# Projecting the neighbourhood queries ahead of keys and values in a two-block transformer kernel

## The chip, the cores and the metric

The kernel runs on one core of a Trainium2 chip, in one launch. The metric is the device time of that launch in microseconds; smaller is better. All arithmetic outside the tables of constants is done on the core, in float32 accuracy.

## The reference

Two transformer blocks follow each other on 256 tokens of width 1024. The first block (two layers) is not touched. The second block also has two layers, and it carries a second stream of 256 context tokens beside `x`. Shortened:

```python
for l in range(DEPTH):                      # 2 layers
    x     = swiglu_half_step(x, ...);  h_ctx = swiglu_half_step(h_ctx, ...)
    hx = modulate(rms_norm(x, ...), ...);  hc = modulate(rms_norm(h_ctx, ...), ...)
    px = hx @ w_in[l]
    pc = hc @ (w_in[l, :, Q_W:] if last else w_in[l])
    qa = rms_norm(heads(px[..., :NA_W]), ...)      # queries of the first kind, 8 heads
    qb = rms_norm(heads(px[..., NA_W:Q_W]), ...)   # of the second kind, 8 heads
    ...                                            # ka, va, kb, vb; the same of pc
    out_a = neighbourhood_attention(qa, ka, va, ka_c, va_c, na_rpb[l])
    out_b = windowed_gqa_attention(qb, kb, vb, kb_c, vb_c, wa_sink[l])
    x = x + mod_x[..., 5, :] * (jnp.concatenate([out_a, out_b], axis=-1) @ w_out[l])
    if not last:                                   # layer 0 alone
        ...                                        # both kinds on the context, into h_ctx
    x = swiglu_half_step(x, ...)
    if not last: h_ctx = swiglu_half_step(h_ctx, ...)
```

In the last layer the context gives keys and values and has no queries.

## The kernel before, in words

**Streams.** `x` and the context `c` are two Python generators, both instances of `stream` (L1511). While the program is recorded a planner (`main`, L1615) steps generators by a modelled clock: each yields a token (a weight product, a wait for an event, a point in time), the planner takes the one that is ready first, and of those ready together the one with the better priority. Smaller pieces run as generators of their own: `head_norm` (L1268) at priority `HN`, and the attention at priority `ATT`, 2 for `x` and 1 for `c`. The order in which they are stepped is the program order of every engine; on the chip nothing is reordered.

**Products.** A weight is loaded as a block `raw` of 128 output columns by 1024 (SyncE's queue), cast on ScalarE to `wh` and its rest kept as `wl` by VectorE (`split`, L148). I call the work on one such block a **unit**: 24 matmuls (8 of wh with the upper part of the activations, 8 of wl, 8 of wh with their lower part). Where both streams need a block at about the same time, one joint unit of 24 matmuls over 512 columns serves both (`together`, L236); otherwise each stream runs its own unit of 256 columns (`alone`, L226), from the same block held in memory. A joint unit takes about as long as two alone.

**The projections of a layer of block 2.** `w_in` has 8 units of queries (4 of the first kind, "kind 0", 4 of the second, "kind 1") and 6 of keys and values, called here by their place in the order of use, #1 to #14. `kv` (L1363) runs the 6 units, and spawns a `head_norm` of the keys; behind these it forms the values of kind 0. `qproj` (L1403) then runs the 4 units of kind 0, spawns their norm, and the 4 of kind 1, and spawns theirs. A head norm is a chain of short steps: squares, sums over heads by small matmuls with `c_heads`, a square root, transposes that spread the factors (`tr`), and for kind 1 of `x` a rotation by `c_rot`.

**Attention.** Behind `kv` a generator `attention` is spawned. It waits for keys and values (for `x` those of both streams), then for the queries of kind 0, runs that kind (`attend`, L829, with `attn2`, L1420), and then kind 1. For one head, ScalarE, VectorE and GpSimd cast keys and queries (`kk`, `qq`), PE forms the scores `ps_s`, ScalarE the exponentials `e` and their sums, PE transposes them (`ps_t`), `pt` copies them, and PE multiplies with the values (`ps_o`). Up to four heads are open (`DEPTH`). Then `w_out` (8 units, #1 to #4 need kind 0 alone) adds to the residual, and the next half step begins with `rms` (L624): sums of squares by small matmuls with `ones`, a square root, a spread, and the scaled activations `hmem`. Its first two units of `w_ffn_up` belong to #45 to #48 of that weight's order of use in the layer.

## Time and profile before

| | before |
|---|---|
| device time, median of 3 runs | 2626.09 us (2618.99 to 2626.55) |
| device time of the profiled execution | 2625.82 us, of which span 2624.0 us |
| TensorE matmul busy | 2491.1 us, 95% of the span |
| VectorE, ScalarE, GpSimd busy | 1743.6, 1046.2, 220.9 us |

The span runs from the first to the last instruction. Times in the trace count from the start of the span. Block 2's first half step and projections of layer 0 end, its attention begins, at about 1283 us; layer 1's attention begins at about 2317 us. "Clock" below is the TensorE clock granted by the throttle, as a share of full speed: 1.00 is 2.4 GHz, the other level is half of it, and a value between them is a mean over the stretch.

### The profile page before, as it was taken

Reading aid. Unit: us, or ns where it says so; the run is one execution under the profiler, and the core shown is the slowest. Engines: PE = TensorE matmul, PEld = TensorE weight load, DVE = VectorE, ACT = ScalarE, POOL = GpSimd, SP = SyncE. Lnnn points to the kernel's source line nnn. Section 1 sums busy time; section 2 is a strip of 40 time slices with the busy share of each in tenths; the row PEclk is TensorE's granted clock in tenths of the full one; section 3 lists DMA queues with packets and bytes.
Section 4 is the critical chain, followed back from the end, with each engine's and each line's share of the span. In section 5 each row is a group of like instructions: output and inputs, shape, how many; then the busy total and the mean of one; then the engine's idle time right before and its main releaser. Section 6 shows DMA issues by size and latency. Waiting matters only on the chain.

```text
span 2624.0 us, 40217 instructions
## 1 busy us (share of the span) xinstructions
PE 2491.1 (95%) x15668; PEld 2239.9 (85%) x15668; DVE 1743.6 (66%) x3255; ACT 1046.2 (40%) x1817; POOL 220.9 (8%) x243
## 2 busy tenths in 40 slices
PE   5989998999998999999989999999999999999999
PEld 4879998989997888889788888888888888988999
DVE  6788887588887765576666757465754445576754
ACT  3555444545443222233566322222322223365543
POOL 2111003121000000000252000000000000041000
PEclk9989998889998999999989899999999999989999
DMA  7776885546763644534311245454354443431564
GB/s 280 248 235 210 287 283 188 180 147 194 232 189 115 192 145 133 155 113 137 106 32 49 85 154 171 118 171 127 114 167 146 128 129 105 129 96 42 174 192 133
DMA packets 127071, 408.92 MB, mean 156 GB/s; under 512 B 15585, under 2 KB 21281, under 8 KB 126753
## 3 DMA queue, kind: packets, MB, share of 16 engines
q1 hardware_dynamic: 126880, 406.35, 49.4%
q8 instruction: 123, 2.02, 0.3%
q14 instruction: 68, 0.55, 0.1%
HBM read 405.22 MB, written 1.07 MB: 155 GB/s over the span
## 4 chain that ended last, share of the span: by engine, by line
PE 75%; DVE 11%; DMA 6%; ACT 4%; issue 3%; POOL 1%; SPq 0%; ACTq 0%; DVEq 0%; POOLq 0%
PE ps_mm L131 65%; PE ps_o L131 3%; PE ps_s L131 3%; DMA raw<-in_w_ffn_in 3%; DVE wl L149 3%; PE ps_t L136 2%; PE ps_t L131 2%; DVE junk L456 2%; ACT wh L149 1%; DMA raw<-in_w_ffn_out 1%; DVE hmem L653 1%; DVE tr L650 1%; DMA adaw<-in_w_ada 1%; POOL tr L475 1%; ACT e L785 1%
## 5 line engine op out<-in xcount | busy, mean ns | idle before, releaser
L131 PE MATMUL ps_mm<-hmem,wh 128*128 128x256 f32 (+1 forms) x5760 | 1386.3, 331 | 49.8 <-ACT hmem L473 21.6
L131 PEld LDWEIGHTS ps_mm<-hmem,wh 128*128 128x128 f32 x5760 | 997.0, 195 | 159.3 <-ACT hmem L473 22.0
L131 PE MATMUL ps_mm<-hmem,wl 128*128 128x256 f32 (+2 forms) x2880 | 950.9, 330 | 2.1 <-DVE wl L149 2.0
L149 ACT CAST wh<-raw 128x1024 fp32r<-128x1024 f32 (+2 forms) x572 | 546.0, 958 | 867.8 <-PE ps_mm L131 371.7
L149 DVE TENSOR_TENSOR wl<-raw,wh 128x1024 fp32r<-128x1024 f32 (+2 forms) x556 | 625.5, 1128 | 355.6 <-ACT wh L149 353.4
L131 PEld LDWEIGHTS ps_mm<-hmem,wl 128*128 128x128 f32 x2880 | 558.9, 194 | 49.9 <-DVE wl L149 2.9
L131 PE MATMUL ps_mm<-g,wh 128*128 128x256 f32 (+1 forms) x2328 | 534.1, 323 | 3.8 <-ACT g L149 3.8
L456 DVE SCALAR_TENSOR_TENSOR junk<-adaw,cb 128x1024 fp8e4<-128x1024 f32 x343 | 423.1, 1233 | 27.8 <-DMA adaw<-in_w_ada 23.3
L131 PEld LDWEIGHTS ps_mm<-g,wh 128*128 128x128 f32 x2328 | 393.0, 191 | 37.5 <-ACT g L149 4.0
L131 PE MATMUL ps_mm<-g,wl 128*128 128x256 f32 (+1 forms) x1164 | 375.3, 322 | 2.5 <-DVE wl L149 2.5
L131 PEld LDWEIGHTS ps_mm<-g,wl 128*128 128x128 f32 x1164 | 222.9, 191 | 19.3 <-DVE wl L149 2.9
L965 POOL TENSOR_TENSOR kk<-kT,kk 64x512 fp32r<-64x512 f32 (+1 forms) x30 | 35.7, 1189 | 1359.6 <-ACT kk L964 1358.5
L735 DVE TENSOR_TENSOR tr<-tr,ps_mm 128x512 f32<-128x512 f32 x61 | 42.0, 688 | 144.9 <-PE ps_mm L131 144.9
L734 ACT ACTIVATE tr<-ps_mm 128x512 f32<-128x512 f32 x61 | 36.5, 598 | 242.6 <-PE ps_mm L131 242.6
L756 DVE SCALAR_TENSOR_TENSOR x_res<-ps_mm,ada_x,x_res 128x256 f32<-128x256 f32 x144 | 67.0, 481 | 92.0 <-PE ps_mm L131 91.5
L131 PEld LDWEIGHTS ps_o<-g,pt 128*128 128x128 f32 x808 | 109.4, 207 | 11.2 <-ACT pt L371 7.4
L131 PE MATMUL ps_o<-g,pt 128*128 128x64 f32 (+1 forms) x808 | 111.8, 287 | 4.8 <-ACT pt L371 4.5
L785 ACT ACTIVATE e<-e,small 128x256 f32<-128x256 f32 (+2 forms) x160 | 90.7, 568 | 34.9 <-DVE small L779 33.8
L131 PE MATMUL ps_mm<-wh,hmem 128*128 128x256 f32 x512 | 94.1, 282 | 0.0
L136 PE MATMUL ps_t<-c_ident,e 128*128 128x128 f32 x404 | 69.8, 297 | 12.9 <-ACT e L785 5.8
L131 PEld LDWEIGHTS ps_mm<-wh,hmem 128*128 128x128 f32 x512 | 79.5, 188 | 0.6 <-ACT g L371 0.6
L149 ACT CAST g<-tr 128x256 fp32r<-128x256 f32 (+1 forms) x137 | 68.3, 499 | 25.2 <-DVE tr L681 10.9
(227 smaller groups left out, 2034.5 us busy)
## 6 DMA issues: line engine op xcount, KB each, us to landing
adaw<-in_w_ada SPq DMA_DIRECT2D x231, 512.0 KB, 4.4
raw<-in_w_ffn_up SPq DMA_DIRECT2D x176, 512.0 KB, 3.9
raw<-in_w_ffn_in SPq DMA_DIRECT2D x88, 512.0 KB, 4.6
raw<-in_w_ffn_down SPq DMA_DIRECT2D x96, 384.0 KB, 3.1
raw<-in_w_ffn_out SPq DMA_DIRECT2D x48, 384.0 KB, 4.0
raw<-in_w_in SPq DMA_DIRECT2D x28, 512.0 KB, 3.7
raw<-in_w_in_ab SPq DMA_DIRECT2D x16, 512.0 KB, 6.6
raw<-in_w_o SPq DMA_DIRECT2D x16, 512.0 KB, 4.8
```

What stands on the lines that cost most here:

```text
L131: self.tc.keep_in_program_order(self.nc.tensor.matmul(out, left, right, start=start, stop=stop))
L136: self.tc.keep_in_program_order(self.nc.tensor.transpose(out, in_, self.ident))
L149: return (self.nc.scalar.copy(hi, src), (eng or self.nc.vector).tensor_tensor(out=lo, in0=src, in1=hi.bitcast(F32), op=OP.subtract))
L456: ins = self.nc.vector.scalar_tensor_tensor(out=self.junk, in0=raw, scalar=1.0, in1=v, op0=OP.mult, op1=OP.mult, accum_out=acc[:, j:j + 1] ...
L475: nc.gpsimd.tensor_scalar(out=h32[:, j, :], in0=src[:, j, :], scalar1=a[:, k0 + j:k0 + j + 1], scalar2=b[:, k0 + j:k0 + j + 1], op0=OP.mul ...
L650: nc.vector.scalar_tensor_tensor(out=t[:, j, :], in0=x[:, k + j, :], scalar=a[:, k + j:k + j + 1], in1=bc, op0=OP.mult, op1=OP.mult)
L653: nc.vector.scalar_tensor_tensor(out=hl[:, k + j, :T], in0=t[:, j, :], scalar=b[:, k + j:k + j + 1], in1=hh[:, k + j, :T].bitcast(F32), op ...
L734: nc.scalar.activation(sg, job.full[0], AF.Silu)
L735: nc.vector.tensor_tensor(out=sg, in0=sg, in1=job.full[1], op=OP.mult)
L756: self.nc.vector.scalar_tensor_tensor(out=x[:, k, :], in0=ps[j], scalar=gate[:, k:k + 1], in1=x[:, k, :], op0=OP.mult, op1=OP.add)
L785: nc.scalar.activation(e[:, at:at + w], e[:, at:at + w], AF.Exp, bias=nm, scale=-1.0, accum_out=sm)
L965: self.nc.gpsimd.tensor_tensor(out=there, in0=k, in1=here.bitcast(F32), op=OP.subtract)
```

## The change

`qproj` takes the kind as an argument and projects that kind's 4 units only. `stream` calls it for kind 0 ahead of `kv`, and for kind 1 behind it, where the attention's generator has been spawned. The context of layer 1, which has no queries, skips both. The event `free`, on which attention pages wait, is set by `stream` behind the second call. No unit is added or taken away: in every shape the two programs have the same number of weight products.

```diff
@@ -1400,22 +1400,20 @@
         self.store[("v", th, l)] = (va, vb)
         self.events.add(("v", th, l))
 
-    def qproj(self, th, l):
-        self.store[("q", th, l)] = qs = []
-        for kind in range(2):
-            for ci in range(2):
-                job = yield from self.products(th, ("w_in_2", l), (4 * kind + 2 * ci, 4 * kind + 2 * ci + 1), self.h_mv,
-                                               ((0, KT),), l == 0)
-                sb = self.page("g")
-                if not job.full:
-                    self.copy(back(sb), rows(job.bank))
-                else:
-                    for j in range(2):
-                        self.copy(back(sb[:, j:j + 1, :]), rows(job.outs[j][:, None, :]))
-                qs.append(sb)
-            self.spawn(self.head_norm([(q, 2 * kind, kind == 1 and th == "x") for q in qs[2 * kind:]], l,
-                                      ("q", th, l, kind), True), HN)
-        self.events.add(("free", th, l))
+    def qproj(self, th, l, kind):
+        qs = self.store.setdefault(("q", th, l), [])
+        for ci in range(2):
+            job = yield from self.products(th, ("w_in_2", l), (4 * kind + 2 * ci, 4 * kind + 2 * ci + 1), self.h_mv,
+                                           ((0, KT),), l == 0)
+            sb = self.page("g")
+            if not job.full:
+                self.copy(back(sb), rows(job.bank))
+            else:
+                for j in range(2):
+                    self.copy(back(sb[:, j:j + 1, :]), rows(job.outs[j][:, None, :]))
+            qs.append(sb)
+        self.spawn(self.head_norm([(q, 2 * kind, kind == 1 and th == "x") for q in qs[2 * kind:]], l,
+                                  ("q", th, l, kind), True), HN)
 
     def attn2(self, th, l, box, kind):
 
@@ -1516,8 +1514,11 @@
             yield from self.ffn2(th, x, l, 0, True)
             yield ("need", ("x", l, 3))
             h = yield from self.rms(th, x, P(4), P(3), covered=True)
+            last = th == "c" and l == 1
+            if not last:
+                yield from self.qproj(th, l, 0)
             yield from self.kv(th, h, l)
-            if th == "c" and l == 1:
+            if last:
                 return
             box = {}
 
@@ -1530,7 +1531,8 @@
                     yield from self.attend(self.attn2(th, l, box, kind), ("att", th, l, kind), ("free", th, l))
 
             self.spawn(attention(), ATT[th])
-            yield from self.qproj(th, l)
+            yield from self.qproj(th, l, 1)
+            self.events.add(("free", th, l))
             yield ("need", ("x", l, 5))
             yield ("need", ("att", th, l, 0))
 
```

In the program order the change is seen at three places. All three are TensorE's (PE's) rows. `ps_mm<-hmem,wh` and `wl` are products of units, `ps_s` scores, `ps_t<-c_ident,e` transposes of exponentials, `ps_t<-c_ident,tr` and `c_heads` steps of a head norm.

Layer 0, before: the last unit of the queries of kind 1 (#14, `ps_mm_12643`) and the first scores.

```order
L131 MATMUL ps_mm_12643<-hmem,wh_12646 128x512 x2
L131 MATMUL ps_mm_12643<-hmem,wl_12647 128x512
L131 MATMUL ps_mm_12643<-hmem,wh_12646 128x512
L131 MATMUL ps_s_12662<-kk_12635,qq_12638 128x512 x2
L136 MATMUL ps_t_12680<-c_ident,e_12620 128x128 x4
L136 MATMUL ps_t_12687<-c_ident,e_12626 128x128 x4
L131 MATMUL ps_s_12694<-kk_12635,qq_12638 128x512 x2
L131 MATMUL ps_mm_12643<-hmem,wh_12646 128x512
L131 MATMUL ps_mm_12643<-hmem,wl_12647 128x512
```

Now the last unit of kind 1 (`ps_mm_12597`), and the first scores of all:

```order
L131 MATMUL ps_mm_12597<-hmem,wl_12601 128x512
L131 MATMUL ps_mm_12597<-hmem,wh_12600 128x512 x2
L131 MATMUL ps_mm_12597<-hmem,wl_12601 128x512
L131 MATMUL ps_mm_12597<-hmem,wh_12600 128x512
L131 MATMUL ps_s_12660<-kk_12636,qq_12639 128x256 x4
L131 MATMUL ps_t_12686<-c_heads_7393,tr_12645 128x2 x4
L131 MATMUL ps_t_12686<-c_heads_7393,tr_12648 128x2 x4
L131 MATMUL ps_s_12709<-kk_12670,qq_12673 128x256 x4
L131 MATMUL ps_s_12727<-kk_12719,qq_12722 128x256 x4
L131 MATMUL ps_s_12745<-kk_12737,qq_12740 128x256 x4
L136 MATMUL ps_t_12763<-c_ident,e_12661 128x128 x4
```

Before, the scores of the first two heads (of 512 columns, `x`'s) stand ahead of and within the last unit; now no score stands ahead of its end, and the first are the context's (256 columns). Ahead of it, between the four units of kind 1, now stand the transposes of the keys' norm. From there to row 5906 of PE's order there is no unit at all: the context's heads run alone, and the first unit of `w_out`, the context's, is at row 5907. In the order before, only attention stands in PE's rows 5869 to 5956.

Layer 0, before: the end of the last `w_out` unit and the first `w_ffn_up` unit; `ps_t<-ones` are the sums of the two streams' `rms`.

```order
L131 MATMUL ps_mm_14467<-hmem,wl_14436 128x256
L131 MATMUL ps_mm_14467<-hmem,wh_14435 128x256
L131 MATMUL ps_t_14496<-ones,acc_14364 128x1
L131 MATMUL ps_t_14496<-ones,tr_14465 128x1 x2
L131 MATMUL ps_t_14496<-ones,acc_14364 128x1
L131 MATMUL ps_t_14496<-ones,tr_14465 128x1 x2
L131 MATMUL ps_t_14518<-ones,acc_14229 128x1
L131 MATMUL ps_t_14518<-ones,tr_14494 128x1 x2
L131 MATMUL ps_t_14518<-ones,acc_14229 128x1
L131 MATMUL ps_t_14518<-ones,tr_14494 128x1 x2
L136 MATMUL ps_t_14540<-c_ident,small_14506 128x128 x2
L131 MATMUL ps_mm_14575<-hmem,wh_14578 128x256
```

Now the same sums of `x`; `ps_mm_14610` is a unit of `w_ffn_up` for the context, which has run ahead:

```order
L131 MATMUL ps_mm_14610<-hmem,wh_14613 128x256 x2
L131 MATMUL ps_mm_14610<-hmem,wl_14614 128x256
L131 MATMUL ps_mm_14610<-hmem,wh_14613 128x256
L131 MATMUL ps_t_14641<-ones,acc_14513 128x1
L131 MATMUL ps_t_14641<-ones,tr_14608 128x1 x2
L131 MATMUL ps_t_14641<-ones,acc_14513 128x1
L131 MATMUL ps_t_14641<-ones,tr_14608 128x1 x2
L131 MATMUL ps_mm_14610<-hmem,wh_14665 128x256
L131 MATMUL ps_mm_14610<-hmem,wl_14666 128x256
```

Before, both streams' sums and spreads stand between the last `w_out` unit and the first `w_ffn_up` unit. Now four units of the context (PE's rows 6336 to 6408) surround `x`'s sums, and `x`'s own four units follow.

Layer 1, before: the end of the last query unit (`ps_mm_21112`), the end of the context keys' norm, and the first scores.

```order
L131 MATMUL ps_mm_21112<-hmem,wl_21158 128x256
L131 MATMUL ps_mm_21112<-hmem,wh_21157 128x256
L136 MATMUL ps_t_21187<-c_ident,tr_21150 128x128 x2
L136 MATMUL ps_t_21187<-c_ident,tr_21188 128x128 x2
L131 MATMUL ps_t_21216<-c_heads_7393,tr_21196 128x2 x4
L131 MATMUL ps_t_21216<-c_heads_7393,tr_21199 128x2 x4
L131 MATMUL ps_s_21239<-kk_21208,qq_21211 128x512 x2
L131 MATMUL ps_s_21245<-kk_21208,qq_21211 128x512 x2
L131 MATMUL ps_s_21263<-kk_21255,qq_21258 128x512 x2
L131 MATMUL ps_s_21281<-kk_21255,qq_21258 128x512 x2
L136 MATMUL ps_t_21287<-c_ident,e_21240 128x128 x4
L136 MATMUL ps_t_21294<-c_ident,e_21246 128x128 x4
```

Now the same place:

```order
L131 MATMUL ps_mm_21116<-hmem,wh_21163 128x256
L136 MATMUL ps_t_21193<-c_ident,tr_21154 128x128 x2
L136 MATMUL ps_t_21206<-c_ident,tr_21194 128x128 x2
L136 MATMUL ps_t_21212<-c_ident,tr_21207 128x128 x2
L131 MATMUL ps_t_21216<-c_heads_7393,tr_21200 128x2 x4
L131 MATMUL ps_t_21216<-c_heads_7393,tr_21203 128x2 x4
L131 MATMUL ps_s_21253<-kk_21245,qq_21248 128x512 x2
L131 MATMUL ps_s_21259<-kk_21245,qq_21248 128x512 x2
L131 MATMUL ps_s_21277<-kk_21269,qq_21272 128x512 x2
L136 MATMUL ps_t_21297<-c_ident,tr_21295 128x128 x2
L136 MATMUL ps_t_21297<-c_ident,tr_21298 128x128 x2
L131 MATMUL ps_s_21307<-kk_21269,qq_21272 128x512 x2
```

In both, all scores stand behind the last query unit and the end of the keys' norm. What is new is the pair of transposes of `tr_21295` and `tr_21298`, the norm of the queries of kind 1, between the scores of the second head and ahead of the transposes of the first exponentials. Further on the two orders are nearly the same.

ScalarE's order has 6 more casts of `qq` (102 for 96) and 2 more of `kk`; GpSimd's has 3 more memsets, 3 more subtractions for `qq` and 2 more for `kk`.

## Rows read from the trace of the kernel before

**Rows 1.** The page: busy time, share of the span, instructions by engine.

```profile
PE 2491.1 (95%) x15668; PEld 2239.9 (85%) x15668; DVE 1743.6 (66%) x3255; ACT 1046.2 (40%) x1817; POOL 220.9 (8%) x243
```

**Rows 2.** Windows, layer 0: stretch and length, PE, PEld, DVE, ACT, POOL busy, clock, DMA share, GB/s.

```profile
1172.00:1198.00 26.00, 23.21 (x168) 21.89 (x168) 23.96 (x54) 12.47 (x23) 0.00 (x0) 0.93 0.29 93
1283.00:1295.00 12.00, 10.04 (x41) 7.74 (x40) 7.40 (x16) 4.52 (x11) 0.16 (x2) 0.86 0.46 152
1295.00:1306.00 11.00, 10.98 (x69) 9.38 (x68) 3.96 (x11) 10.12 (x22) 6.52 (x10) 1.00 0.17 38
1306.00:1318.00 12.00, 10.40 (x68) 9.38 (x67) 7.73 (x28) 9.12 (x27) 7.54 (x13) 0.80 0.06 17
1318.00:1338.00 20.00, 17.03 (x121) 16.13 (x122) 9.70 (x34) 15.23 (x43) 10.23 (x18) 0.87 0.05 11
1338.00:1352.00 14.00, 11.80 (x74) 10.02 (x72) 9.72 (x25) 11.48 (x32) 8.82 (x12) 0.88 0.10 26
...
1366.00:1464.00 98.00, 94.96 (x707) 89.19 (x707) 68.27 (x165) 53.82 (x130) 16.30 (x28) 0.97 0.19 58
1464.00:1490.00 26.00, 21.55 (x120) 19.57 (x119) 22.59 (x63) 12.69 (x23) 0.00 (x0) 0.68 0.14 42
1283.00:1464.00 181.00, 169.10 (x1184) 155.27 (x1183) 118.00 (x301) 112.08 (x280) 58.30 (x93) 0.93 0.17 51
```

**Rows 3.** Timeline, PE, the hand-over at 1464 us: start, duration, operation, idle before.

```profile
1469.26 0.66 PE L136 MATMUL ps_t<-c_ident,small 128*128 128x128 f32 x2 [1.02 <-DVE small L354]
1471.03 0.58 PE L131 MATMUL ps_mm<-hmem,wh 128*128 128x256 f32 x1 [1.11 <-ACT hmem L652]
```

**Rows 4.** Lines by shape, ACT, 1290 to 1464 us: count, busy, mean ns, idle before.

```profile
L972 ACT CAST qq<-g 64x256 fp32r<-64x256 f32 x58 | 23.3, 403 | 5.7 <-PE ps_s L131 4.8
...
L785 ACT ACTIVATE e<-e,small 128x256 f32<-128x256 f32 x32 | 16.0, 499 | 1.8 <-DVE small L779 1.6
...
L785 ACT ACTIVATION_READ_ACCUMULATOR e<-e,small 128x1 f32 x64 | 12.0, 187 | 0.0
...
L1301 ACT COPY tr<-small 128x256 f32<-128x256 f32 x8 | 2.7, 401 | 2.5 <-DVE small L359 2.5
...
L964 ACT CAST kk<-kT 64x512 fp32r<-64x512 f32 x7 | 4.3, 617 | 2.3 <-PE ps_s L131 2.2
L964 ACT CAST kk<-kT 64x256 fp32r<-64x256 f32 x10 | 4.0, 402 | 2.8 <-PE ps_s L131 2.6
...
L371 ACT COPY pt<-ps_t 128x512 f32<-128x512 f32 x24 | 13.9, 577 | 16.1 <-PE ps_t L136 16.1
...
L149 ACT CAST wh<-raw 128x1024 fp32r<-128x1024 f32 x8 | 8.4, 1048 | 14.3 <-PE ps_mm L131 14.2
L149 ACT CAST hmem<-ps_t 128x512 fp32r<-128x512 f32 x8 | 4.6, 579 | 8.8 <-PE ps_t L136 8.8
...
L1283 ACT ACTIVATE tr<-g 128x256 f32<-128x256 f32 x6 | 2.2, 408 | 0.0
...
L785 ACT ACT_TABLE_LOAD x1 | 1.3, 1283 | 0.0
```

**Rows 5.** The same view for PE, of the same stretch.

```profile
L131 PE MATMUL ps_o<-g,pt 128*128 128x64 f32 x384 | 51.6, 284 | 0.6 <-ACT pt L371 0.6
...
L136 PE MATMUL ps_t<-c_ident,e 128*128 128x128 f32 x192 | 31.1, 294 | 2.2 <-ACT pt L371 1.7 <-DVE hmem L149 0.3
...
L131 PE MATMUL ps_s<-kk,qq 128*128 128x256 f32 x64 | 14.3, 342 | 3.0 <-ACT qq L972 1.3 <-POOL qq L974 1.0 <-POOL kk L965 0.4
```

**Rows 6.** Windows, layer 1: the start of the attention.

```profile
2317.00:2345.00 28.00, 22.79 (x110) 19.08 (x109) 14.88 (x34) 15.34 (x37) 10.37 (x15) 0.70 0.25 71
```

**Rows 7.** Timeline, PE, the same start.

```profile
2322.17 1.05 PE L131 MATMUL ps_t<-c_heads,tr 128*128 128x2 f32 x8 [1.59 <-ACT tr L1283]
...
2328.47 1.36 PE L136 MATMUL ps_t<-c_ident,e 128*128 128x128 f32 x8 [1.35 <-ACT e L785]
2331.36 1.12 PE L136 MATMUL ps_t<-c_ident,tr 128*128 128x128 f32 x4 [1.53 <-ACT tr L1301]
```

## The prediction

> **What bounds the kernel now.** I read the page first, then the windows about the stages that the change touches, then the timeline of their gaps. The page shows PE busy in 95% of the span, and no other engine in over 66% but PE's own weight loads [rows 1]. The two programs hold the same number of weight products in every shape, so the change can win or lose only what PE loses beside its work. I count that per stretch as a **loss**: the time in which PE is not busy, plus (1 − clock) times the length, for the time that a lowered clock costs. The windows give three places where a loss can move [rows 2, 6]:
>
> - the attention of layer 0, 1283 to 1464 us: 11.9 us not busy, and by the clocks of the stretches in it 0.14 × 12 + 0.20 × 12 + 0.13 × 20 + 0.12 × 14 + 0.03 × 98 = 11.3; **23.2 in all**;
> - the hand-over behind it, 1464 to 1490: 26 − 21.55 = 4.45, and 0.32 × 26 = 8.3; **12.8 in all**;
> - the start of the attention in layer 1, 2317 to 2345: 5.2, and 0.30 × 28 = 8.4; **13.6 in all**.
>
> In the hand-over the reader is to see a chain without cover: both streams end their `w_out` together, so PE stands behind a square root for 1.02 us, behind the first `hmem` for 1.11 [rows 3], and the clock is 0.68 over the stretch. In layer 1 it is PE waiting for ScalarE, three times 1.35 to 1.59 us within ten [rows 7], and the clock is 0.70.
>
> A measurement of this kernel tells about 0.3% (7.9 us) from no change: the three runs shown lie within that.
>
> **The change, part by part.**
>
> *Its stated aim.* The four units of kind 1 were to run beside the first attention. The order of PE doesn't have it so. In layer 0 the first scores now stand behind the last of those units (before, two heads' scores stood ahead of its end); what stands between the units is the keys' norm, which before was over by then. In layer 1 scores stood behind all units and still do. I give the aim nothing.
>
> *Hand-over, layer 0: −8.2.* In the new order the context's attention comes first, so its `w_out` and `rms` are done early, and four `w_ffn_up` units of the context stand around `x`'s sums. The trace has this pattern once: at 1172 to 1198 four units of one stream lie around the other's sums, and the loss there is 2.79 + 0.07 × 26 = 4.6 [rows 2]. So 12.8 falls to about 4.6. Bounds: −12.8 (all hidden) and −4 (half of it comes back, `x`'s own chain being longer than its cover).
>
> *Attention, layer 0: 23.2 becomes some 22.6, so −0.6.* The new order has four parts.
> (a) The context's heads alone, 46 rows of PE with no unit to fill them. ScalarE has there 17 casts of `qq` at 0.403, 16 exponentials at 0.499 + 0.187, 7 `tr` at 0.401, 5 and 4 casts of `kk` at 0.402 and 0.617, 4 `pt` at 0.577, and one each of `wh`, `hmem`, L1283 and a table load (1.048, 0.579, 0.408, 1.283): 30.8 us [rows 4]. PE has 64 transposes at 31.1/192 = 0.162, 32 scores at 14.3/64 = 0.223, 32 `ps_o` at 51.6/384 = 0.134 [rows 5], 21.8, and 28 rest, some 5: about 27. ScalarE is the longer one. In the rows where it is busiest it reaches 10.12 of 11 us and 11.48 of 14 [rows 2], 0.92 and 0.82. At 0.82 the part takes 37.5 us, a loss of 10.5; I take 10. Bounds: 4 (ScalarE never waits) and 26 (PE at the pace of layer 1's start, 14.4 useful us of 28 [rows 6]: 27/0.51 = 53).
> (b) The context's first four `w_out` units with the first heads of `x` and the context's kind 1: PE has enough to do, as in 1295 to 1306 (loss 0.02) [rows 2]. I take 1, between 0 and 3.
> (c) PE's rows 5993 to 6060, heads of both streams without a unit: by the same prices ScalarE 36, PE 36. At 0.92 it takes 39 us, at 0.82 44: a loss of 3 to 8, and I take 6.5. At the pace of 1306 to 1318 (loss 1.6 + 2.4 of 12 [rows 2]) it would take 53, a loss of 17.
> (d) The rest, 55 us of PE's work with eight units among it, like 1366 to 1464, which loses 3.0 + 2.9 in 98 us [rows 2]: 3.4. The last four units of `w_out` lose some 0.7.
> (e) Ahead of the first scores, the units with the keys' norm between them. Before, 1283 to 1295 lost 2.0 + 1.7 [rows 2]; four joint units cover such a chain better, so I take 1.
> Sum: 10 + 1 + 6.5 + 3.4 + 0.7 + 1 = 22.6. With all low bounds it is some 9, with all high ones some 50.
>
> *A new wait in the projections of layer 0: +1.2.* The sums of the first queries' norm now stand in a unit that the context runs alone, behind squares which wait behind a weight cast on ScalarE (1.048 [rows 4]), and PE keeps its program order. Bounds 0 and 3; the nearest row is one cast.
>
> *Layer 1: −1.* The first three heads' `qq` can now be cast early, which takes part of the 1.35 and 1.59 us waits away [rows 7]. Against it, two transposes of the norm of kind 1 stand ahead of the transposes of the first exponentials and wait for ScalarE behind a table load and three exponentials (1.283 + 3 × some 0.7, about 3.5 us). Bounds −6 and +5; what is saved and what is added are each about 3 us, so I take little.
>
> *Doubled casts.* 6 `qq` and 2 `kk`, about 0.4 us each, 3.2 in all on ScalarE. Those in (a) are in its sum; the others lie where ScalarE is busy 53.8 of 98 us [rows 2] and cost nothing. Without that cover it would be 3 us.
>
> *Joint and alone units.* Some units of `w_out` and `w_ffn_up` change from joint to alone in layer 0, as many of `w_in` the other way in layer 1: counts are equal in every shape, so nothing.
>
> **Sum:** −8.2 − 0.6 + 1.2 − 1 = −8.6 against the profiled execution's 2625.82, so **2617**. That execution stands 0.3 us below the median of the runs, so the median gives the same.
>
> **The rivals.**
>
> *A, slower: the starved attention lowers the clock.* Place: parts (a) and (c), in which no unit stands between the heads. If ScalarE's answers leave PE a short gap at every head, the clock falls as at 2317 to 2345 [rows 6]. Then (a) loses 26 and (c) 17, the attention 26 + 1 + 17 + 3.4 + 0.7 + 1 = 49 instead of 23.2, and the sum is −8.2 + 26 + 1.2 − 1 = +18, or 2644. It decides once the attention loses over 39 us. For it: 1306 to 1318 has clock 0.80 and no unit of weight [rows 2]. Against it: the old order has such a stretch too and its clock was 0.80 to 0.88, never 0.70. The Trainium skill, "TensorE: Matmul & The Clock Gate", section "A second HAM failure mode: psum-queue depth-cycling", says that frequent short idles of PE between groups of matmuls make its clock swing between the two levels, and that throughput suffers though single matmuls look full; it speaks against taking the units out from between the heads. By that rule the sum is this rival's; the trace agrees as far as the 0.70 of the stretch with three gaps of about 1.5 us goes.
>
> *B, no difference: the saving is given back.* (a) and (c) run between my value and A's: (a) loses 15, (c) 10, the attention 31, +8. The sum is 0: 2626, give or take 4. For it: ScalarE and PE are about even in (a) and (c), and when two engines alternate neither is ever full.
>
> *C, the aim works after all:* the units of kind 1 fill the starved starts in both layers. The losses at 1306 to 1318 and 1338 to 1352 (4.0 + 3.9) and of layer 1 (13.6) go beside the 8.2: −30 (8.2 + 7.9 + 13.6), or 2596. Against it: the program order, which the chip can't change.
>
> **How the numbers follow.** The forecast gets 0.55, its own range 2608 to 2624: 0.42 of it lies below 2618, 0.13 above. B gets 0.27, all of it within 0.3%. A gets 0.11, all slower. C gets 0.07, all faster. So faster 0.49, the same 0.40, slower 0.11. The range leaves out most of A and of C: 2603 to 2632.
>
> **What would show it.** Right: PE's loss in the 26 us behind the attention falls from 12.8 to about 5, and the first `w_ffn_up` products of the context surround the sums of `x`; the stretch of the context's heads shows ScalarE at 0.8 or more and a clock of 0.8 to 0.9; layer 1's start still has gaps ended by ScalarE, one of them ahead of transposes of the second norm. Wrong: a clock near 0.7 in the context's stretch (A), scores beside units of kind 1 (C), or a hand-over that still loses 10 us since `x`'s `hmem` comes later than four units last.

## The result, and the profile after

The change makes the kernel slower: 2645.15 us (median of 4 runs, 2644.73 to 2647.69) against 2622.54 for the kernel before (4 runs, 2617.31 to 2626.55), a ratio of 1.0114 with a 95% interval of 1.0093 to 1.0135. The two medians alone give 1.0086, so the size of the loss is known to some 23 to 30 us. The profiled execution took 2644.73 us, with a span of 2642.9. Forecast were 2617 and a range that ended at 2632. The page of the change, busy time by engine, to lay beside [rows 1]:

```profile
span 2642.9 us, 40230 instructions
...
PE 2500.9 (95%) x15668; PEld 2249.0 (85%) x15668; DVE 1735.7 (66%) x3251; ACT 1049.6 (40%) x1821; POOL 223.9 (8%) x251
```

PE has 10 us more on its count for the same 15668 matmuls, at a clock of 0.96.

To see where the time went, I cut both traces at the same places. All matmuls up to the 7121st are the same in both programs; it starts at 1165.99 us before and at 1161.49 after. The second cut is the spread of layer 1's first `rms` in block 2 (1843.3 and 1861.7 us). Between them lie the first score, and the end of the last transposes of an attention output (`osb`):

| us | before | changed | difference |
|---|---|---|---|
| start to the 7121st matmul (same order) | 1165.99 | 1161.49 | −4.5 |
| to the first score of layer 0 | 127.71 | 135.29 | +7.6 |
| to the last `osb` transposes of layer 0 | 155.96 | 184.97 | +29.0 |
| to layer 1's first `rms` | 393.63 | 379.95 | −13.7 |
| from there to the end of the last matmul | 776.27 | 776.77 | +0.5 |

So layer 0 lost 22.9 us and layer 1 nothing; the 4.5 us at the start are chance, as the instructions there are the same. Windows of the change in the parts of the forecast (stretch and length; PE, PEld, DVE, ACT, POOL busy; clock; DMA share; GB/s), against [rows 2, 6]:

```profile
1168.00:1194.00 26.00, 21.90 (x145) 20.45 (x144) 22.34 (x52) 12.62 (x25) 0.00 (x0) 0.87 0.32 101
1274.00:1296.80 22.80, 21.58 (x102) 17.30 (x100) 13.13 (x29) 9.21 (x21) 3.63 (x5) 1.00 0.39 122
1296.80:1340.20 43.40, 34.41 (x208) 31.91 (x207) 27.87 (x87) 31.25 (x86) 19.81 (x30) 0.76 0.09 30
1340.20:1371.40 31.20, 26.33 (x192) 24.78 (x190) 10.78 (x30) 13.20 (x37) 10.22 (x18) 0.89 0.05 13
1371.40:1417.40 46.00, 40.61 (x263) 36.61 (x262) 22.79 (x67) 30.19 (x79) 24.29 (x36) 0.82 0.09 22
1417.40:1470.00 52.60, 51.77 (x408) 50.02 (x406) 38.06 (x90) 28.45 (x60) 6.66 (x12) 0.96 0.18 61
1470.00:1486.00 16.00, 10.98 (x55) 10.44 (x55) 8.75 (x23) 4.80 (x11) 0.00 (x0) 0.58 0.01 2
1486.00:1512.00 26.00, 25.37 (x210) 24.80 (x210) 21.61 (x51) 12.64 (x21) 0.00 (x0) 1.00 0.29 92
2337.00:2365.00 28.00, 21.53 (x135) 17.82 (x133) 17.52 (x42) 15.07 (x34) 11.77 (x13) 0.82 0.23 70
```

In the forecast's measure (time not busy plus (1 − clock) times the length), row by row:

| part | forecast | measured |
|---|---|---|
| alone stretch with the new wait (1168) | 4.6 + 1.2 | 4.1 + 3.4 = 7.5 |
| (e) the keys' norm between the units (1274) | 1 | 1.2 |
| (a) the context's heads alone (1296.8) | 10 | 9.0 + 10.4 = 19.4 |
| (b) with the context's first `w_out` units (1340.2) | 1 | 4.9 + 3.4 = 8.3 |
| (c) heads of both streams (1371.4) | 6.5 | 5.4 + 8.3 = 13.7 |
| (d) the rest, with the last `w_out` units (1417.4, and 1470 to 1486) | 3.4 + 0.7 | 0.8 + 2.1, and 5.0 + 6.7 = 14.6 |
| hand-over (1486) | 4.6 | 0.6 |

The hand-over did better than forecast (12.8 before). The attention, (a) to (e), lost 57.2 in place of 23.2 before, 26.3 of it idle time (11.9 before) and 30.9 the clock's share (11.3 before), and so gave back nearly three times what the hand-over won. Two kinds of gaps are to be seen. In (a), PE waits between heads (timeline of PE: start, duration, operation, idle before and what ended it):

```profile
1303.69 1.34 PE L131 MATMUL ps_s<-kk,qq 128*128 128x256 f32 x4 [3.53 <-ACT qq L972]
...
1320.02 1.09 PE L136 MATMUL ps_t<-c_ident,e 128*128 128x128 f32 x4 [2.16 <-DVE small L354]
```

And at the end of (d), a wait that the forecast did not have at all:

```profile
1470.51 0.61 PE L136 MATMUL ps_t<-c_ident,e 128*128 128x128 f32 x4
1475.61 1.09 PE L136 MATMUL ps_t<-c_ident,e 128*128 128x128 f32 x4 [4.50 <-ACT hmem L652]
```

VectorE in the same microseconds:

```profile
1471.05 1.27 DVE L653 SCALAR_TENSOR_TENSOR hmem<-tr,ada_c,hmem 128x256 fp32r<-128x256 f32 x3
1472.24 1.25 DVE L650 SCALAR_TENSOR_TENSOR tr<-c_res,ada_c,ps_t 128x256 f32<-128x256 f32 x3
1473.41 1.27 DVE L653 SCALAR_TENSOR_TENSOR hmem<-tr,ada_c,hmem 128x256 fp32r<-128x256 f32 x3
1474.60 0.86 DVE L650 SCALAR_TENSOR_TENSOR tr<-c_res,ada_c,ps_t 128x256 f32<-128x256 f32 x2
1475.38 0.68 DVE L369 COPY pt<-ps_t 128x512 f32<-128x512 f32 x1
```

The transposes of `x`'s last exponentials need one of the two PSUM buffers `ps_t`. One holds the spread of the context's `rms`, which the products of L650 read until the last of them ends at 1475.46 (1474.60 + 0.86); the other holds the transposes of the head before, and their copy `pt` stands behind those products in VectorE's order, at 1475.38. PE goes on at 1475.61. So it stood for 4.50 us behind the context's `rms`, whose `hmem` on ScalarE the profile names, and the clock of 1470 to 1486 is 0.58.

### The profile page after: what moved, and what is told of

It is laid out like the page before. It is cut to its first block, busy times and chain, and to the rows that moved or that the text cites. A ratio compares the mean times of both kernels' runs of the same rounds, so it can differ in the third digit from the quotient of the medians.

```text
span 2642.9 us, 40230 instructions
## 1 busy us (share of the span) xinstructions
PE 2500.9 (95%) x15668; PEld 2249.0 (85%) x15668; DVE 1735.7 (66%) x3251; ACT 1049.6 (40%) x1821; POOL 223.9 (8%) x251
## 4 chain that ended last, share of the span: by engine, by line
PE 72%; DVE 9%; DMA 4%; ACT 3%; issue 2%; POOL 1%; ACTq 0%; SPq 0%; DVEq 0%; POOLq 0%
PE ps_mm L131 62%; PE ps_o L131 3%; PE ps_t L136 2%; PE ps_s L131 2%; DVE wl L149 2%; DMA raw<-in_w_ffn_in 2%; PE ps_t L131 2%; DVE junk L456 1%; DMA adaw<-in_w_ada 1%; DMA raw<-in_w_ffn_out 1%; ACT wh L149 1%; DVE tr L650 1%; DVE hmem L653 1%; ACT e L785 1%; POOL tr L475 0%
## 5 line engine op out<-in xcount | busy, mean ns | idle before, releaser
L456 DVE SCALAR_TENSOR_TENSOR junk<-adaw,cb 128x1024 fp8e4<-128x1024 f32 x343 | 421.5, 1229 | 29.5 <-DMA adaw<-in_w_ada 24.7
L131 PEld LDWEIGHTS ps_mm<-g,wl 128*128 128x128 f32 x1164 | 222.9, 192 | 19.4 <-DVE wl L149 2.9
L974 POOL TENSOR_TENSOR qq<-g,qq 64x256 fp32r<-64x256 f32 x51 | 43.5, 852 | 1271.4 <-ACT qq L972 1269.1
L785 ACT ACTIVATE e<-e,small 128x512 f32<-128x512 f32 (+2 forms) x160 | 90.8, 568 | 37.0 <-DVE small L779 35.8
L136 PEld LDWEIGHTS ps_t<-c_ident,e 128*128 128x128 f32 x404 | 52.4, 161 | 34.3 <-ACT e L785 9.8
```

The costliest lines, as they stand in the source:

```text
L131: self.tc.keep_in_program_order(self.nc.tensor.matmul(out, left, right, start=start, stop=stop))
L136: self.tc.keep_in_program_order(self.nc.tensor.transpose(out, in_, self.ident))
L456: ins = self.nc.vector.scalar_tensor_tensor(out=self.junk, in0=raw, scalar=1.0, in1=v, op0=OP.mult, op1=OP.mult, accum_out=acc[:, j:j + 1] ...
L785: nc.scalar.activation(e[:, at:at + w], e[:, at:at + w], AF.Exp, bias=nm, scale=-1.0, accum_out=sm)
L974: self.nc.gpsimd.tensor_tensor(out=qq[p0:p0 + 64, 1, :], in0=q, in1=qq[p0:p0 + 64, 0, :].bitcast(F32), op=OP.subtract)
```

## The experiments

Each table row below is cut as above; "score" is from the 7121st matmul to the first score, "heads" from there to the last `osb` transposes, "rest" to layer 1's `rms`, "layer 1" from there to the end of the last matmul, all of the one profiled execution; the times are medians. A ratio is to runs of the kernel before that were made along with that run, with medians of 2617.18 to 2622.54; a difference of medians between two rows of the table can carry a few microseconds of that.

| run | median us | ratio to before, 95% interval | score | heads | rest | layer 1 |
|---|---|---|---|---|---|---|
| before | | | 127.7 | 156.0 | 393.6 | 776.3 |
| the change | 2645.15 | 1.0114 (1.0093 to 1.0135) | 135.3 | 185.0 | 380.0 | 776.8 |
| layer 0 alone | 2640.02 | 1.0075 (1.0046 to 1.0103) | 135.3 | 179.4 | 379.1 | 774.6 |
| layer 1 alone | 2621.46 | 1.0012 (0.9995 to 1.0030) | 126.2 | 150.9 | 393.2 | 778.3 |
| `x` first | 2640.27 | 1.0079 (1.0049 to 1.0109) | 135.4 | 173.7 | 380.8 | 779.0 |
| tail | 2638.34 | 1.0073 (1.0047 to 1.0099) | 135.3 | 173.1 | 381.1 | 777.0 |
| filler | 2650.53 | 1.0119 (1.0082 to 1.0156) | 136.0 | 186.0 | 379.4 | 779.1 |
| six heads | 2629.13 | 1.0039 (1.0024 to 1.0054) | 135.3 | 164.3 | 379.7 | 779.5 |
| keys' norm in two | 2620.22 | 1.0005 (0.9989 to 1.0021) | 122.3 | 176.3 | 379.2 | 774.1 |
| keys' norm in two, tail | 2612.67 | 0.9977 (0.9960 to 0.9993) | 121.8 | 170.6 | 380.3 | 770.7 |
| keys, kind 0, values, kind 1 | 2606.16 | 0.9955 (0.9930 to 0.9979) | 112.1 | 173.5 | 380.7 | 769.7 |
| the same, layer 0 alone | 2615.67 | 0.9981 (0.9969 to 0.9993) | 114.2 | 174.5 | 380.6 | 776.6 |
| that order, keys' norm in two | 2602.18 | 0.9943 (0.9924 to 0.9963) | 112.8 | 172.5 | 380.7 | 767.1 |
| the same, six heads | 2631.68 | 1.0050 (1.0031 to 1.0070) | 117.7 | 189.9 | 391.8 | 764.5 |

"Score" and "heads" are read together where units stand beside the heads: an earlier first score lengthens the second and shortens the first.

### Which layer

For layer 0 alone:

```diff
-            if not last:
+            if not last and l == 0:
                 yield from self.qproj(th, l, 0)
...
+            if not (l == 0):
+                yield from self.qproj(th, l, 0)
             yield from self.qproj(th, l, 1)
```

and the same with `l == 1`.

> The split of the queries is made in layer 0 only; layer 1 projects both kinds behind keys and values as before. My theory (all of the loss lies in layer 0's attention: the context's heads run first and alone, with nothing beside them): 18 to 26 us slower than before, ratio 1.007 to 1.010. Rival (the loss lies in layer 1, where keys and values are now joint units that wait for both streams): within 5 us of before.

> The split of the queries in layer 1 only. My theory (layer 1 takes no part in the loss): layer 0 takes what it took before (674 to 680 us from the anchor ahead of its projections to layer 1's first rms), layer 1 773 to 778, the total within 6 us of before. Rival (joint units of keys and values in layer 1 make x wait for the context): layer 1 over 780, 5 to 15 us slower.

Layer 0 alone is slower by 0.75%, as its theory had it; layer 1 alone is 2621.46, 3.4 us above its runs of before, with an interval about 1. The loss is layer 0's. Its stages lay outside of what was expected for them: layer 0 took 670.2 us, layer 1 778.3. The layer 1 run does something else for the reader: up to layer 1, PE's order in it is that of the kernel before, row for row, so that its attention is a second look at [rows 2]. Its windows of the attention and of the hand-over:

```profile
1283.00:1457.00 174.00, 161.15 (x1181) 147.44 (x1180) 117.70 (x300) 111.87 (x280) 58.45 (x93) 0.98 0.18 52
1457.00:1483.00 26.00, 21.08 (x127) 18.92 (x127) 22.50 (x63) 12.69 (x23) 0.00 (x0) 0.80 0.19 56
```

The clock here is 0.98 and 0.80, where the execution of before had 0.93 and 0.68, though the gaps are the same ones (1.55, 2.33, 1.36 and 1.27 us in the attention; before 1.55, 2.34, 1.36 and 1.28). Layer 0 took 670.2 us here and 677.3 there. Seven microseconds of the profiled execution of before were the clock's chance, and stages of one execution carry that uncertainty. It also shows that a higher clock over the same rows is time won.

### The context first, or heads without units

```diff
-                for s in ("xc" if th == "x" else "c"):
+                for s in "xc":
...
-ATT = {'x': 2, 'c': 1}
+ATT = {'x': 1, 'c': 2}
```

> The change, but the context's attention waits for x's keys too, and x has the better priority, so that x's heads come first in layer 0 and the context's stand beside w_out units. My theory (starving comes from the context's heads being first and alone): the loss of the attention falls by 10 to 20 us, so 2625 to 2635. Rival (any heads without a unit beside them starve alike, whichever stream is first, and the first heads still have none): no better than the change, 2640 to 2650.

2640.27, at the edge of the rival's range and outside the theory's. The heads' stretch was 11 us shorter in the profiled execution, which is the theory's size, but the first 43.4 us from the first score are little better than in the change:

```profile
1297.40:1340.80 43.40, 37.00 (x212) 32.67 (x211) 28.02 (x70) 26.18 (x62) 20.84 (x29) 0.76 0.19 43
```

Clock 0.76, as in the change's (a), PE not busy for 6.4 us against 9.0. It isn't the context alone that starves: whichever stream is first starves without units beside its heads.

### The tail

```diff
-            h = yield from self.rms(th, x, P(g0 + 1), P(g0), covered=s == 0 and l == 1)
+            h = yield from self.rms(th, x, P(g0 + 1), P(g0), covered=s == 0 and l == 1,
+                                    gate=("att", "x", l, 1) if th == "c" and s == 1 else None)
...
+        if gate is not None:
+            yield ("need", gate)
         bc = self.p("t", (128, 256))
```

> The change, with one move: the context's scaled activations (the second rms of layer 0) are written only when x's attention has ended, so that VectorE doesn't write them ahead of the last copy of x's transposed exponentials. My theory: the wait of 4.5 us there and the lowered clock behind it go, 6 to 11 us faster than the change, 2634 to 2639, and the four covering units still cover. Rival (the activations then come too late for the units that need them): the hand-over loses what the tail gains, 2643 to 2648.

2638.34, 6.8 below the change, as the theory had it, though the intervals of the two ratios overlap. The traces show the gain by itself: PE's rows are the same up to the last heads, and from the end of (c) to the last `osb` transposes 64.1 us became 56.2. (The other 4.0 us by which the heads' stretch is shorter lie in (c), ahead of the move, at another clock.) Windows about the end of `x`'s attention and of the hand-over behind it:

```profile
1455.00:1471.40 16.40, 15.30 (x120) 14.22 (x119) 8.87 (x30) 6.31 (x16) 0.61 (x2) 0.97 0.00 1
1471.40:1497.00 25.60, 24.25 (x195) 23.97 (x194) 22.31 (x53) 13.12 (x22) 0.00 (x0) 0.95 0.32 93
```

The gap of 4.5 us is gone, the clock is 0.97 where the change had 0.58, and the four covering units still cover: 1.4 us not busy in the 25.6 us behind.

### What paces the heads: the clock, ScalarE, or the heads open

The filler:

```diff
+            if th == "c" and kind == 0:
+                self.filler(vs[0][0][0], 3)
             yield self.lat("soft")
             pt = self.turn(e)
+            if th == "c" and kind == 0:
+                self.filler(vs[0][0][0], 3)
...
+    def filler(self, v, n):
+        at = self.clock
+        ps = self.p("mm", (128, 512))
+        for _ in range(n):
+            self.mul(ps[:, :128], v[:, 0, 0:128], v[:, 0, 0:128])
+        self.clock = at
```

> The change, with 3 matmuls of 128 columns, whose result nobody reads, behind the scores and behind the transposes of every head of the context's kind 0 in both places that one head waits: 48 in all, some 10 us of PE's work put where PE stands idle for 9.0 us; the rest of PE's order is the change's. My theory (half of the loss in the context's stretch, 10.4 of 19.4 us, is the lowered clock and follows from the short gaps): the clock of the stretch rises from 0.76 to over 0.9 and the stretch stays at 40 to 44 us though PE has 10 us more to do. Rival (the heads are bound by ScalarE's chain, whatever PE's clock): the clock rises and the stretch stays the same too, but ScalarE is busy over 0.9; or (the filler only delays) the stretch takes 50 us or more at the old clock.

```profile
1305.70:1350.00 44.30, 39.08 (x302) 36.91 (x301) 26.75 (x86) 31.62 (x85) 20.09 (x29) 0.94 0.10 30
```

The clock rose from 0.76 to 0.94, and the stretch from the first score to the first `w_out` unit took 44.9 us instead of 43.5, with the 48 more matmuls in it (96 rows of the trace, two for each):

```profile
L131 PE MATMUL ps_mm<-g 128*128 128x128 f32 x96 | 14.4, 291 | 0.0
```

ScalarE is no limit: it is busy for 31.62 of 44.3 us, 0.71, about the 0.72 of the change. Neither of the rival's two branches came out whole; the theory's clock came, and its length but for 0.9 us. By itself the run doesn't price the clock, since the filler takes time too. Only part of it went into the gaps: PE's idle time fell from 9.0 to 5.2 us. The rest was made up by PE's own matmuls, which took less time at the higher clock: they are busy for 30.7 us in place of 34.5.

Two other runs price the clock without a filler. In "layer 0 alone" the rows of PE in layer 0 are those of the change, in "tail" they are so up to the last heads, and by chance their clocks differ. The first line is (a) in "layer 0 alone", the second (c) in "tail", each cut at the same rows as in the change:

```profile
1297.10:1337.40 40.30, 30.76 (x209) 28.01 (x208) 28.18 (x87) 31.53 (x87) 20.09 (x30) 0.85 0.11 32
1372.90:1415.20 42.30, 36.78 (x263) 32.69 (x263) 22.70 (x67) 30.03 (x79) 24.31 (x36) 0.92 0.10 24
```

(a) took 40.3 us at a clock of 0.85, in the change 43.4 at 0.76; PE is idle for 9.5 us there and for 9.0 in the change. (c), between these rows, took 42.3 us at 0.92, in the change 46.2 at 0.82, with 5.5 and 5.4 us idle. So the waits stay and PE's matmuls get shorter: of the clock's share, 4.4 us less in (a) and 4.9 less in (c), 3.1 and 3.9 came back as time. Taken to all of the 10.4 us, some 7 us of (a) are the clock's price; that is an estimate from these two. The 9.0 us of idle time are the other part. There PE waits five times, 0.67 to 3.53 us long, for steps of ScalarE and VectorE, four heads being open at most (one that counts as open is a head of the context, or half the queries of a head of `x`). The next run was to try that number, on the premise that PE's clock doesn't pace the stretch, which the two lines above don't bear out. Six heads:

```diff
+    def depth(self):
+        return 6 if self.phase == ("x", 0) else DEPTH
...
-            start = bool(todo) and self.open_units < DEPTH
+            start = bool(todo) and self.open_units < self.depth()
```

(and so at the two other places where `DEPTH` is read)

> The change, with up to six heads open at once in layer 0 of block 2 instead of four. What the filler left open: what paces the context's stretch, when neither PE's clock nor a full ScalarE does. Theory (the length of the chain of one head, over the number of heads open): the stretch from the first score to the first w_out unit falls by 5 to 12 us. Rival (program order on ScalarE and the two PSUM banks per kind of tile pace it): within 3 us of the change's 43.5, and the total within 6 us of the change.

The total fell by 16 us to 2629.13, and the heads' stretch from 185.0 to 164.3. The stretch to the first `w_out` unit itself grew from 43.5 to 50.5, since heads of `x` now stand in it (nine pairs of score matmuls of 512 columns in PE's order ahead of that unit, before four). So the theory's number failed, and the rival's did too. The gain lies behind the first 43.4 us: in these the clock is still 0.76, with ScalarE at 0.80, and in the 40.6 us behind them it is 1.00, where the change had 0.89 and 0.82.

```profile
1296.00:1339.40 43.40, 36.19 (x220) 32.70 (x218) 27.12 (x88) 34.56 (x93) 23.70 (x34) 0.76 0.08 22
1339.40:1380.00 40.60, 37.54 (x310) 35.94 (x310) 22.33 (x65) 27.05 (x73) 22.36 (x38) 1.00 0.12 33
```

Over the whole stretch PE's idle time fell from 25.1 to 18.0 us and the clock rose from 0.85 to 0.93; at its end PE still waits, 4.21 us, now ahead of the last `osb` transposes. That more open heads shorten this attention is shown. That it is by the length of one head's chain over the number of heads open is not: the order of all heads and units changed with it.

### Why the units of kind 1 were not beside the first attention

```diff
                 keep(2 * i + j, job, j)
+        self.spawn(self.head_norm([(kT[i][:, s:s + 1, :], 1, False) for i in range(4)], l, ("k0", th, l), False), HN)
...
-        self.spawn(self.head_norm([(kT[i][:, s:s + 1, :], 1 if i < 4 else 3, i == 4 and th == "x") for i in range(5)],
+        self.spawn(self.head_norm([(kT[4][:, s:s + 1, :], 3, th == "x")],
...
-                    yield ("need", ("k", s, l))
+                    yield ("need", ("k0", s, l))
...
+                    if kind == 1:
+                        for s in ("xc" if th == "x" else "c"):
+                            yield ("need", ("k", s, l))
```

> The change, with the keys' norm in two: the four tiles of kind 0 are normed on their own as soon as they are projected, the fifth tile (kind 1's, which for x is rotated) after them, and the attention of kind 0 waits for the first norm only. In the order the first scores then stand within the first unit of kind 1, not behind the last. My theory (it was the keys' norm, now last of the three, that kept the first attention behind the units of kind 1): the stage from the first score to the last head falls back and the total lies below before, 2600 to 2615. Rival (heads starve wherever they stand, since ScalarE can't feed PE): still above before, 2625 to 2640.

2620.22: 25 us below the change, but level with before, not below it. With units between the first heads, the first 43.4 us from the first score read:

```profile
1290.30:1333.70 43.40, 40.34 (x254) 35.27 (x253) 26.89 (x70) 38.71 (x100) 26.46 (x39) 1.00 0.31 98
```

PE busy for 40.3 us and the clock 1.00, with ScalarE at 0.89, where in the change's (a) it was at 0.72. The keys' norm did hold the first attention back. Two gaps stand against the rest of what was hoped for: 3.68 us at 1253 us, where transposes of the keys' norm now wait for `tr` (L1301), and the tail again (timeline of PE of this run):

```profile
1257.02 0.66 PE L136 MATMUL ps_t<-c_ident,tr 128*128 128x128 f32 x4 [3.68 <-ACT tr L1301]
...
1460.52 1.09 PE L136 MATMUL ps_t<-c_ident,e 128*128 128x128 f32 x4 [3.66 <-ACT hmem L652]
```

With the tail's repair as well:

> The change with the keys' norm in two and the context's scaled activations behind the end of x's attention, so both repairs together. My theory (the two losses are separate): 4 to 10 us faster than the run with the keys' norm in two, 2610 to 2616, and the gap of 3.7 us at the end of x's attention is gone. Rival (the tail is only moved): the same as that run, about 2620.

2612.67, 7.5 below the run without it, and the gap is gone: the two losses are separate.

Another order of units has the same aim and needs no split norm: keys, kind 0, values, kind 1.

```diff
-            if not last:
-                yield from self.qproj(th, l, 0)
-            yield from self.kv(th, h, l)
+            yield from self.kv(th, h, l, not last)
             if last:
                 return
+            yield from self.qproj(th, l, 0)
+            yield from self.vals(th, h, l)
```

where `vals` is the second half of `kv`, from the first `toks` on.

> Another order of the same units: keys, queries of kind 0, values, queries of kind 1, with attention spawned ahead of the last. The first scores then stand ahead of the third-last unit of kind 1 in layer 0 and heads of both streams stand between these units. My theory (the aim of the change is sound, but the keys' norm has to be over before the units of kind 1 begin): the start of the attention loses little, the hand-over is covered too, 2595 to 2612. Rival (ScalarE limits the heads, so units beside them only move the wait to later heads): only the hand-over's 8 to 12 us are saved, 2612 to 2620, or nothing.

> Keys, queries of kind 0, values, queries of kind 1 in layer 0 only, layer 1 as before. If the 6.5 us that the run with this order in both layers gained from layer 1's first rms to the end are real, that stage is back at 774 to 777 us and layer 0 keeps its gain of 11: 2608 to 2614 in total. Rival (they were chance): that stage is at 768 to 772 here as well.

2606.16, faster than before by 0.45%, and 2615.67 with layer 0 alone, whose layer 1 is back at 776.6 as expected, though its total lies 1.7 us above the expected range: so both layers gain, the second 6.8 us. Now both norms are over when kind 1 begins, and the first 43.4 us from the first score are nearly full:

```profile
1277.10:1320.50 43.40, 41.93 (x268) 36.30 (x266) 26.11 (x69) 35.09 (x92) 24.12 (x35) 1.00 0.27 85
```

The version with the lowest median joins that order with the keys' norm in two:

> Keys, queries of kind 0, values, queries of kind 1, in both layers, and the keys' norm in two. In layer 0 the order of PE from the second pair of values on is that of the run with this order of units, so layer 0 stays at 664 to 672 us; if the keys' norm in two also helps layer 1, that stage falls to 764 to 769. Total 2600 to 2608; it would be the fastest version. Rival (the first attention has all that it needs already): the same as the run with this order alone, 2606, give or take 4.

2602.18, 0.57% faster than before. It lies in its theory's range and in its rival's too, and its interval overlaps with that of the order alone, so what the split norm adds there isn't shown. And the last run put six heads on top of it:

> The fastest version so far with up to six heads open in layer 0 as well. In its order both streams now end their w_out together again, so that both sums of squares stand ahead of the first w_ffn_up unit, as in the kernel before. My theory (each of the two is worth what it showed alone): the attention gains up to 8 us, since its heads have units beside them here already, and the hand-over loses 8 to 12 again: 2602 to 2612, no faster than the version with four heads. Rival (open heads are what counts, with or without units): the attention gains the 20 us that it gained over the change, 2590 to 2596.

2631.68: slower by 29 us than with four heads, so both theories missed. The hand-over's part came as forecast (the rest is 11.1 us longer, and PE again waits behind the sums of both streams), but the heads' stretch did not shorten, it grew by 17.4. Its windows of the first 43.4 us from the first score and of the hand-over:

```profile
1286.00:1329.40 43.40, 36.98 (x190) 32.40 (x189) 21.54 (x56) 29.95 (x81) 25.16 (x37) 0.80 0.23 72
1484.00:1510.00 26.00, 22.99 (x147) 21.41 (x146) 22.97 (x66) 10.90 (x20) 0.00 (x0) 0.74 0.27 81
```

With four heads PE is busy for 41.93 of the first 43.4 us at a clock of 1.00, here for 36.98 at 0.80. Why more open heads hurt there, when they helped in the change, was not tried further and stays open.

## Why the prediction was wrong

- **The aim.** Right: the first scores stood behind the last unit of kind 1, and nothing of the aim came. What stood in the way was named ("what stands between the units is the keys' norm"), and splitting it gave 25 us back.
- **Hand-over, −8.2.** Right in its mechanism, and 12.2 in size: the loss fell from 12.8 to 0.6. The four units covered more than the stretch at 1172 us from which I took 4.6.
- **Attention, "23.2 becomes some 22.6".** This step failed. Measured by the same count it became 57.2 (the sum of (a) to (e) in the table above), +14.4 in idle time and +19.6 in the clock's share. (a) and (c) were priced by ScalarE's largest share, 0.82 to 0.92, as if ScalarE paced the heads; it was busy for 0.72 of (a) and 0.66 of (c). ScalarE's work was right (30.8 forecast, 31.25 measured), the pace was not: with no unit between the heads PE waited for single steps of ScalarE and VectorE, and the sum had no term for the clock that fell over these waits, to 0.76 in (a) and 0.82 in (c). For (b) I took a stretch with whole units between the heads as its measure, and 31 us with four 256-column units are not that: 8.3 in place of 1. PE's rows in (a) were miscounted, 64 transposes and 32 `ps_o` where the trace has 40 and 64; at the same prices that is 15.1 us in place of 14.7, so nothing hung on it.
- **(d), 3.4, and 0.7.** 11.7 of its 14.6 are the tail. I followed PE's order and priced ScalarE's, but did not look at VectorE's order, where the copy now stood behind the context's `rms`. The cover of the hand-over and the tail are one and the same move: the context's chain is early, so its writes come amid `x`'s last head.
- **New wait, +1.2.** 1.73 us of idle time, in size near, but at another row: PE waited for a weight's `wl`, not for the squares, as the timeline of PE in the change shows:

```profile
1180.99 0.38 PE L131 MATMUL ps_mm<-hmem,wl 128*128 128x256 f32 x1 [1.73 <-DVE wl L149]
```

With the clock the stretch lost 2.9 more than the one at 1172 us of the kernel before.
- **Layer 1, −1.** +0.5, within its bounds. The wait that I put at 3.5 us stands there, at the row named, in the timeline of PE:

```profile
2343.54 0.44 PE L136 MATMUL ps_t<-c_ident,tr 128*128 128x128 f32 x2 [1.61 <-ACT tr L1301]
...
2347.67 1.19 PE L131 MATMUL ps_s<-kk,qq 128*128 128x512 f32 x2 [0.72 <-DVE small L356]
2352.28 1.11 PE L136 MATMUL ps_t<-c_ident,tr 128*128 128x128 f32 x4 [3.42 <-ACT tr L1301]
```

The clock of that stretch is 0.82 instead of 0.70 [rows 6], and the two even out.

- **Joint and alone units, doubled casts: nothing.** Nothing was seen of them: the rest of layer 0 behind the hand-over, and layer 1 from its first `rms` on, take the same.
- **The rivals.** A came; it had 0.11. Its place, parts (a) and (c), its mechanism and its number, 2644, were right, its sizes less so: the clock fell to 0.76 and 0.82 where it had 0.70, and the parts lost 19.4 and 13.7 where it had 26 and 17. That the clock costs time there is shown by the same rows at other clocks. The number is in part luck: the tail's 11.7, which A did not have, fills what (a) and (c) fell short, and the greater gain of the hand-over and 4.5 us of chance at the start pull the other way. The rule of the Trainium skill that I weighed there ("TensorE: Matmul & The Clock Gate", section "A second HAM failure mode: psum-queue depth-cycling") says that frequent short idles of PE go with a clock that swings between its levels, and with less throughput. The trace agrees in both: (a) has its gaps and a clock of 0.76, and took 43.4 us for what took 40.3 at 0.85. B and C did not come.

The measure itself, idle time plus the clock's share, held: over the parts of layer 0 in the table it rose by 24.7, and the stages of layer 0 by 22.9 us. What was wrong is what I filled in for stretches without cover.

## What to carry to other kernels

Taking work away from between chains that wait on one another can't be priced by the busy share of the engine that looks fullest: the waits of each chain count, and the lower clock that came with them here. A stretch without cover is best compared with one that has as little of it. A filler that raises the clock doesn't show what the clock costs, since it takes time itself; the same rows in another execution, at another clock, do. When a norm or another chain gates the work that a reordering is to overlap, look at which chain ends last in the new order: here the keys' norm, not the queries', and the order keys, first queries, values, second queries ends both in time. When one stream's chain is moved early to cover another's, look at every engine's queue at the place where it now lands, not at the one that it was meant to cover.

## What was not expected of the hardware

- The same instructions with the same gaps got a clock of 0.93 in one execution and 0.98 in another over the attention, 0.68 and 0.80 over the hand-over, 7 us in all. A clock term taken from one execution is partly chance.
- A lowered clock costs time even where PE also waits for other engines: the same rows took 43.4 us at 0.76 and 40.3 at 0.85, with 9.0 and 9.5 us idle.
- 48 matmuls put where PE waits raised the granted clock from 0.76 to 0.94 and lengthened the stretch by 1.4 us.
